# Gate and up weights of an expert: four transfers of 2 MB become two of 4 MB, with five slots recut in the second expert

## The chip, the cores and the metric

The kernel runs on one core of one Trainium2 chip. The metric is the device time of one execution in microseconds (us). Three runs of the kernel before gave 1424.24, 1423.74 and 1421.06 us; their median is 1423.74 us.

## What is computed

Two transformer blocks on 256 tokens of width 1024, all in float32. The first block has a mixer of two head groups, then a mixture of experts, then a gated projection; the second has a local attention, a recurrent branch and a feed-forward part. The change touches only the mixture of experts:

```python
def moe(u, w_router, b_router, w_gu, b_gu, w_dn, b_dn):   # top 4 of 32 experts per token
    logits = jnp.dot(xt, w_router) + b_router
    top_logit, top_e = lax.top_k(logits, TOP_K)
    gate = jax.nn.softmax(top_logit, axis=-1)
...
    def expert_block(args):
        e, xs = args
        hh = jnp.dot(xs, w_gu[e]) + b_gu[e]                # w_gu[e] is 1024 x 2048, 8 MB
        glu, lin = jnp.split(hh, 2, axis=-1)
        glu = jnp.minimum(glu, SWIGLU_LIMIT)
        lin = jnp.clip(lin, -SWIGLU_LIMIT, SWIGLU_LIMIT)
        act = glu * jax.nn.sigmoid(SWIGLU_ALPHA * glu) * (lin + 1.0)
        return jnp.dot(act, w_dn[e]) + b_dn[e]             # w_dn[e] is 1024 x 1024, 4 MB
```

Every expert's 12 MB of weights are read once from HBM, 384 MB for the 32 experts.

## The kernel before

All weights, from the first projection to the last, come through one list, `plan` (L176 to L218), filled by `want(key, source, shape)`. An entry is a chunk of at most 2 MB: 128 partitions with 16 KB each. A chunk needs a slot of 16 KB per partition. There are ten slots: ring `a` has three, which live through the whole kernel, `b0` to `b4` have one each and live from the end of the attention (`cb`) to the end of the experts, and `c` and `d` have one each during the experts. `load_next(ring)` (L222) takes the next entry of the plan and issues its transfer on SP's DMA queue into a tile of that ring; `done(key)` (L255) is called in the code behind the last matmul that reads a chunk, and loads the next entry into the ring that the chunk had. SP executes its transfers in order; each waits, by semaphores, for the matmuls that still read the slot, and for the transfer eight before it on the same semaphore.

In the experts an entry `("gu", e, c)` is a quarter of the gate and up weights of expert e (two row blocks of 2048 columns, in one run of 16 KB per partition), `("dn", e, c)` a half of the down weights. The plan's order is gu of expert e, then dn of expert e-1. The last six transfers of the experts keep out of ring `a` (L226), so that its three slots take the weights of the next stage (`pg`, `in2`) as soon as the plan is there. Ring `d` is given up after expert 10, since the path for overfull experts (`past_slots`) and a table for the second block use its memory.

PE's order in the experts is written out by hand (`manual_schedule`, L1210): `up(e+1)`, that is four quarters of 16 matmuls each, with the scatter of expert e-1 behind the first two and the gates of expert e+2 behind the third; then the first half of `down_part(e)`, the transposes of `glu(e+1)` (tile `tr`), the gather of the tokens of expert e+2 (tile `xg`), and the second half of `down_part(e)`. ACT and DVE do the activation between. This hand-written order ends behind `up(E - 1)`; the last calls of `down_part` and `glu` are placed by a scheduler:

```python
        h1 = up(e + 1, aside)
        if e == E - 2:
            break
...
    order.close()
    i = down_part(E - 2, aT, 0)
    with tc.issue_after(i.ins):
        aL = glu(E - 1, h1)
    down_part(E - 2, aT, 1)
    down_part(E - 1, aL, 0)
    i = down_part(E - 1, aL, 1)
```

In the rows, tile `gu` is the PSUM result of `up` (L1086), `y` that of `down_part` (L1122, one PSUM bank), `w` any weight chunk, `gl` the activation that `down_part` reads, `h` the copy of `gu` that the transposes read. A quarter of `up` is 16 matmul records, a half of `down_part` too.

Of the kernel before, what the change touches and what calls it, by code (L numbers as in the profile page):

```python
# [25 lines left out]
FT = mybir.dt.float32  # L26
# [10 lines left out]
P = 128  # L37
S = 256
D = 1024
E = 32  # L40
# [64 lines left out]
def block_kernel(ctx: ExitStack, tc: tile.TileContext, A, out, dbg=None, parts=("t1", "moe", "over", "t3")):  # L105
# [70 lines left out]
    plan = []  # L176

    def want(key, ap, shape):
        plan.append((key, ap, shape))
# [10 lines left out]
    want(("o", 0), wo[0], [P, 4, 1024])  # L190
    fd = dram.tile([8, 384], FT, name="fd")
    wg, wd = A["w_gu"], A["w_dn"]
    for e in range(E + 1):
        if e < E:
            for c in range(4):
                want(("gu", e, c), wg[e, c], [P, 2, 2048])
                if (e, c) == (1, 0):
                    want(("pp",), A["w_pp"].rearrange("(k p) n -> p k n", p=P), [P, 2, 1024])
        if e > 0:
            for c in range(2):  # L200
                want(("dn", e - 1, c), wd[e - 1, c], [P, 4, 1024])
        if e == E_REL:
            want(("R",), bass.AP(tensor=fd.tensor, offset=fd.offset, ap=[[1, P], [1, 2944]]), [P, 2944])
# [9 lines left out]
    for j in range(11):  # L213
        want(("up", j), A["w_up"][j], [P, 2, 2048])
        if j % 2 == 0:
            n = min(4, 22 - 2 * j)
            want(("down", j // 2), A["w_down"][j * 256:j * 256 + n * P].rearrange("(k p) n -> p k n", p=P),
                 [P, n, 1024])  # L218
    state = {"next": 0, "held": 0, "d": True}
    live = {}  # L220

    def load_next(ring):  # L222
        i = state["next"]
        if i >= len(plan) or (ring != "a" and i >= stop_moe) or (ring == "d" and not state["d"]):
            return
        if ring == "a" and stop_moe - 6 <= i < stop_moe:  # L226

            state["held"] += 1
            return
        state["next"] = i + 1  # L230
        key, ap, shape = plan[i]
        t = rings[ring].tile([P, 4096], FT, name="w")
        n = int(np.prod(shape[1:]))
        v = t[:, :n]
        if len(ap.shape) == 3:
            v = v.rearrange("p (a b) -> p a b", b=ap.shape[2])
        if i == 0:
            for h in range(2):
                SY.dma_start(v[:, h], ap[:, h])
        elif key == ("dn", E - 1, 1):  # L240
            for h in range(2):
                SY.dma_start(v[:, 2 * h:2 * h + 2], ap[:, 2 * h:2 * h + 2])
        else:
            SY.dma_start(v, ap)
        if key == ("R",):
            SY.dma_start(t[0:E, 3072:3072 + D], A["b_dn"])
        live[key] = (t, ring)
        if i + 1 == stop_moe:
            for _ in range(state["held"]):
                load_next("a")  # L250

    def W(key):
        return live[key][0]

    def done(key):  # L255
        load_next(live.pop(key)[1])

    for _ in range(NRING_A):
        load_next("a")
# [749 lines left out]
    held = {}  # L1009
# [167 lines left out]
    def past_slots():  # L1177
# [7 lines left out]
        with tc.If(mv > CAP):  # L1185
            for t in range(2):
# [7 lines left out]
                with tc.For_i(0, E, 1) as e:  # L1194
                    cv = nc.values_load(cnti[0:1, ds(e, 1)], min_val=0, max_val=S)
                    with tc.If(cv > CAP):
                        V.tensor_copy(gc, gover[:, t, ds(e, 1)])
                        V.tensor_copy(bg, bgu[:, ds(e, 1), :].rearrange("p o n -> p (o n)"))
                        for m in range(8):
                            for s in range(2):  # L1200
                                for c in range(4):
                                    G.dma_start(w[:, 2 * c:2 * c + 2],
                                                 wg[ds(e, 1), c, :, :, s * 1024 + m * P:s * 1024 + (m + 1) * P]
                                                 .rearrange("o p k n -> p (o k) n"))
                                for k in range(8):
                                    PE.matmul(pacc[:, s * P:(s + 1) * P], w[:, k], uT[:, k], start=(k == 0), stop=(k == 7))
                            ts(gl, pacc[:, 0:P], bg[:, m:m + 1], 7.0, OP.add, OP.min)
                            act(sg, gl, AF.Sigmoid, scale=1.702)
                            ts(li, pacc[:, P:2 * P], bg[:, 8 + m:9 + m], 7.0, OP.add, OP.min)
                            ts(li, li, -7.0, 1.0, OP.max, OP.add)  # L1210
                            tt(gl, gl, sg, OP.mult)
                            tt(aT[:, m], gl, li, OP.mult)
                        for s in range(8):
                            for c in range(2):
                                G.dma_start(w[:, 4 * c:4 * c + 4], wd[ds(e, 1), c, :, :, s * P:(s + 1) * P]
                                             .rearrange("o p k n -> p (o k) n"))
                            for k in range(8):
                                PE.matmul(pacc[:, 0:P], aT[:, k], w[:, k], start=(k == 0), stop=(k == 7))
                            hs = xn[:, t, s * P:(s + 1) * P]
                            stt(hs, pacc[:, 0:P], gc, hs, OP.mult, OP.add)  # L1220
# [517 lines left out]
def host_arrays(inputs):  # L1738
# [46 lines left out]
    f["g_post_ffn"] = c(g["g_post_ffn_2"])  # L1785
    f["g_pre_ffn"] = c(g["g_pre_ffn_2"])

    f["w_gu"] = c(g["w_gu"][0].reshape(E, 4, 2, P, 2 * D).transpose(0, 1, 3, 2, 4))
    f["w_dn"] = c(g["w_dn"][0].reshape(E, 2, 4, P, D).transpose(0, 1, 3, 2, 4))
    f["b_gu"] = c(g["b_gu"][0].reshape(E, 16, P).transpose(2, 0, 1))  # L1790
    f["b_dn"] = c(g["b_dn"][0])
# [59 lines left out]
```

## Time and profile before

| | |
|---|---|
| median of three runs | 1423.74 us |
| the profiled execution's own time | 1422.5 us |
| its span, first to last instruction | 1420.5 us |
| mean granted TensorE clock | 0.987 of full speed |
| PE busy | 1315.2 us (93%) |
| DVE busy | 627.6 us (44%) |
| ACT busy | 371.8 us (26%) |
| bytes by DMA | 482.40 MB, mean 340 GB/s |

The span is cut into 40 slices of 35.5 us on the profile's page. Slices 1 to 4 are the first block's mixer, the experts fill slices 5 to 30, the second block the rest. PE's share counts every issued matmul as busy for its modelled length, so it says nothing about whether a stage waits for data; the chain of work that ended last says that.

### The profile page before, as it was taken

The numbers are of one execution on the slowest core, as the hardware profiler recorded it, in microseconds if no ns is written. First come the engines' busy times: TensorE is split into PE (matmuls) and PEld (weight loads), VectorE is DVE, ScalarE is ACT, GpSimd is POOL, SyncE is SP. The second block draws the span as 40 slices with busy tenths as digits, with TensorE's granted clock in tenths as the row PEclk, the third lists the DMA queues.
The fourth block names the chain that finished last, engine by engine and source line by source line (L and its number), as shares of the span: only waits on it lengthen the run. The fifth ranks groups of instructions, "written<-read, shape, count | busy, mean of one in ns | idle before, by whom it ended". The sixth has DMA issues, their size and how long they took to land.

```text
span 1420.5 us, 19855 instructions
## 1 busy us (share of the span) xinstructions
PE 1315.2 (93%) x8393; PEld 744.0 (52%) x8394; DVE 627.6 (44%) x1250; ACT 371.8 (26%) x641; POOL 40.0 (3%) x54
## 2 busy tenths in 40 slices
PE   8989999999998888889998888988888998999997
PEld 7777543434333333333343333333335886899997
DVE  6766532332322232222232222322226878677776
ACT  5654211101100010001110001100014658555554
POOL 1010200000000000000000000000000101000000
PEclk9999999999999999999999999999999999999999
DMA  7366899999999999999999999999998523355530
GB/s 287 112 239 270 340 427 427 426 427 426 427 427 427 427 427 426 425 412 427 427 427 427 427 428 427 427 426 427 427 426 350 188 103 134 138 196 197 196 149 31
DMA packets 40591, 482.40 MB, mean 340 GB/s; under 512 B 4104, under 2 KB 4640, under 8 KB 12592
## 3 DMA queue, kind: packets, MB, share of 16 engines
q1 hardware_dynamic: 39232, 477.99, 81.2%
q0 software_dynamic: 832, 2.62, 0.6%
q8 instruction: 68, 1.11, 0.3%
q10 hardware_dynamic: 432, 0.46, 0.1%
q14 instruction: 27, 0.22, 0.0%
HBM read 479.99 MB, written 1.06 MB: 339 GB/s over the span
## 4 chain that ended last, share of the span: by engine, by line
DMA 47%; PE 45%; DVE 4%; issue 2%; ACT 2%; POOL 1%; DVEq 0%; ACTq 0%; SPq 0%; POOLq 0%
DMA w<-w_gu 25%; DMA w<-w_dn 19%; PE gu L1086 10%; PE y L1122 4%; PE acc L289 3%; PE acc L290 3%; PE acc L291 3%; PE wk L290 3%; PE wk L291 3%; PE wk L289 3%; DMA w<-w_pg 2%; PE pj L289 1%; PE pj L291 1%; PE pj L290 1%; PE xg L1056 1%
## 5 line engine op out<-in xcount | busy, mean ns | idle before, releaser
L1086 PE MATMUL gu<-w,xg 128*64 128x512 f32 x2048 | 470.1, 601 | 45.2 <-DMA w<-w_gu 39.1
L1086 PEld LDWEIGHTS gu<-w,xg 128*64 128x64 f32 x2048 | 141.6, 137 | 315.4 <-issue 249.8
L1122 PE MATMUL y<-w,gl 128*64 128x512 f32 x1024 | 233.1, 597 | 28.9 <-DMA w<-w_dn 27.2
L121 ACT ACTIVATE h<-gu,gs 128x512 f32<-128x512 f32 x64 | 40.5, 683 | 558.8 <-PE gu L1086 558.8
L124 DVE TENSOR_TENSOR h<-sc,h 128x512 f32<-128x512 f32 x126 | 81.4, 686 | 201.0 <-PE sc L1146 198.5
L273 DVE TENSOR_TENSOR wl<-w,wh 128x1024 fp32r<-128x1024 f32 (+2 forms) x124 | 147.5, 1200 | 45.5 <-ACT wh L121 45.0
L1122 PEld LDWEIGHTS y<-w,gl 128*64 128x64 f32 x1024 | 73.5, 136 | 161.3 <-issue 157.9
L121 ACT ACTIVATE wh<-w 128x1024 fp32r<-128x1024 f32 (+2 forms) x125 | 128.2, 1038 | 91.0 <-PE acc L291 21.6
L124 DVE TENSOR_TENSOR gl<-tr,bgu 128x512 f32<-128x512 f32 x32 | 22.1, 692 | 270.1 <-PE tr L1101 270.1
L290 PE MATMUL wk<-ul,wh 128*128 128x256 f32 x336 | 94.5, 281 | 0.2 <-DVE ul L124 0.2
L289 PE MATMUL wk<-uh,wh 128*128 128x256 f32 x336 | 94.5, 281 | 0.0
L291 PE MATMUL wk<-uh,wl 128*128 128x256 f32 x336 | 94.3, 281 | 0.0
L121 ACT ACTIVATE sg<-gl 128x512 f32<-128x512 f32 x32 | 20.1, 629 | 183.0 <-DVE gl L131 183.0
L290 PEld LDWEIGHTS wk<-ul,wh 128*128 128x128 f32 x336 | 63.4, 189 | 1.2 <-DVE ul L124 0.4
L1071 DVE CAST gt<-y 128x256 fp32r<-128x256 f32 x32 | 13.6, 424 | 114.0 <-PE y L1069 114.0
L289 PEld LDWEIGHTS wk<-uh,wh 128*128 128x128 f32 x336 | 63.3, 188 | 1.0 <-ACT uh L121 0.2
L291 PEld LDWEIGHTS wk<-uh,wl 128*128 128x128 f32 x336 | 63.4, 189 | 0.0
L1056 PE MATMUL xg<-oh,u 128*128 128x64 bf16 x1536 | 50.0, 193 | 0.7 <-ACT proj L121 0.7
L1056 PEld LDWEIGHTS <-u 128*128 128x128 bf16 x1536 | 49.1, 98 | 2.6 <-issue 2.3
L127 DVE SCALAR_TENSOR_TENSOR cv<-wk,vec,cv 128x255 f32<-128x255 f32 x88 | 42.3, 480 | 8.7 <-ACT cv L121 7.1
L127 DVE SCALAR_TENSOR_TENSOR sg<-y,gs,li 128x512 fp32r<-128x512 f32 x31 | 23.3, 751 | 49.7 <-ACT li L121 49.7
L121 ACT ACTIVATE li<-y,gs 128x512 fp32r<-128x512 f32 x31 | 21.3, 687 | 80.9 <-PE y L1122 79.4
(419 smaller groups left out, 1753.3 us busy)
## 6 DMA issues: line engine op xcount, KB each, us to landing
w<-w_gu SPq DMA_DIRECT2D x128, 2048.0 KB, 39.1
w<-w_dn SPq DMA_DIRECT2D x63, 2048.0 KB, 39.1
w<-w_up SPq DMA_DIRECT2D x11, 2048.0 KB, 7.8
w<-w_in SPq DMA_DIRECT2D x7, 2048.0 KB, 9.5
w<-w_down SPq DMA_DIRECT2D x5, 2048.0 KB, 7.6
w<-w_o SPq DMA_DIRECT2D x4, 2048.0 KB, 8.6
w<-w_pg SPq DMA_DIRECT2D x2, 2048.0 KB, 35.4
w<-w_in SPq DMA_DIRECT2D x2, 1024.0 KB, 8.3
```

What stands on the lines that cost most here:

```text
L121: return SC.activation(out=o, in_=i, func=f, **kw)
L124: return V.tensor_tensor(out=o, in0=a, in1=b, op=op)
L127: return V.scalar_tensor_tensor(out=o, in0=a, scalar=s, in1=b, op0=op0, op1=op1)
L273: eng.tensor_tensor(out=lo, in0=src, in1=hi.bitcast(FT), op=OP.subtract)
L289: PE.matmul(o, l[0], r[0], start=first, stop=False)
L290: PE.matmul(o, l[0], r[1], start=False, stop=False)
L291: PE.matmul(o, l[1], r[0], start=False, stop=last)
L1056: PE.matmul(px[:, kd], u3[i][:, t, kd * P:(kd + 1) * P], oh[:, t], start=(n == 0), stop=(n == 5))
L1071: V.tensor_copy(gt, pgt[:, 0:S])
L1086: PE.matmul(ps[64 * s:64 * s + 64, n], xg[:, k], w[:, kk, s * 1024 + n * 512:s * 1024 + (n + 1) * 512], start=(k == 0), stop=(k == 7))
L1122: i = PE.matmul(ps[64 * s:64 * s + 64], aT[:, k], w[:, kk, s * 512:(s + 1) * 512], start=(k == 0), stop=(k == 7))
```

## The change

- The host lays the gate and up weights out as two halves per expert instead of four quarters. In a half a partition's four row blocks are one run of 32 KB.
- Experts 0 and 1 are still loaded by quarters through the plan (now runs of 16 KB inside the 32 KB). From expert 2 on the plan has only dn; the 60 halves are in a list of their own, `pairs_`.
- Slots `b0` to `b3` are not reloaded when expert 0 is through. Behind the first quarter of expert 1, `cb` is closed, and the memory of the five slots is recut: `p0` and `p1` of 32 KB and a new `b4` of 16 KB. `p0` takes the first halves, `p1` the second ones (`load_pair`). A half's slot comes free when both its quarters are read.
- All other slots take dn. dn of expert e may be loaded once both halves of expert e are issued; until then a free ring is put on the list `wait`, and is loaded behind the next half.
- The rule that kept the last six transfers out of ring `a` is gone.
- The path for overfull experts reads the new layout with half as many transfers. No expert is overfull here, so it does not run.

```diff
-        if e < E:
+        if e < 2:
             for c in range(4):
-                want(("gu", e, c), wg[e, c], [P, 2, 2048])
+                want(("gu", e, c), wg[e, c // 2][:, 2 * (c % 2):2 * (c % 2) + 2], [P, 2, 2048])
...
+        elif e < E:
+            pairs_ += [(e, 0), (e, 1)]
...
+    def load_pair(ring):
+        i = state["pair"]
+        if i >= len(pairs_):
+            return
+        state["pair"] = i + 1
+        e, h = pairs_[i]
+        t = rings[ring].tile([P, 8192], FT, name="w2")
+        SY.dma_start(t.rearrange("p (a b) -> p a b", b=2048), wg[e, h])
+        live["gu", e, 2 * h] = (t[:, 0:4096], None)
+        live["gu", e, 2 * h + 1] = (t[:, 4096:8192], ring)
+        again, state["wait"] = state["wait"], []
+        for r in again:
+            load_next(r)
...
     def load_next(ring):
+        if ring in ("p0", "p1"):
+            return load_pair(ring)
...
-        if ring == "a" and stop_moe - 6 <= i < stop_moe:
-            state["held"] += 1
+        k = plan[i][0]
+        if k[0] == "dn" and k[1] >= 2 and state["pair"] < 2 * (k[1] - 1):
+            state["wait"].append(ring)
             return
...
     def done(key):
-        load_next(live.pop(key)[1])
+        ring = live.pop(key)[1]
+        if ring is None or ring in ("b0", "b1", "b2", "b3"):
+            return
+        if key == ("gu", 1, 0):
+            cb.close()
+            for r in ("p0", "p1", "b4"):
+                rings[r] = pool_(cb, "ring" + r)
+                load_next(r)
+            return
+        load_next(ring)
...
-    f["w_gu"] = c(g["w_gu"][0].reshape(E, 4, 2, P, 2 * D).transpose(0, 1, 3, 2, 4))
+    f["w_gu"] = c(g["w_gu"][0].reshape(E, 2, 4, P, 2 * D).transpose(0, 1, 3, 2, 4))
```

The change moves two things that an argument about time has to look at. The first is SP's queue from expert 0 on. Before (the first `x6` are quarters of experts 0 and 1, the `x4` behind are expert 2, then 3):

```order
L244 DMA w<-w_gu 128x4096 x6
L244 DMA w<-w_dn 128x4096 x2
L244 DMA w<-w_gu 128x4096 x4
L244 DMA w<-w_dn 128x4096 x2
L244 DMA w<-w_gu 128x4096 x4
```

That is: the four quarters of expert e+1 always stand ahead of the two dn of expert e. In the changed kernel, on the same queue and from the same place:

```order
L265 DMA w<-w_gu 128x4096 x6
L265 DMA w<-w_dn 128x4096 x2
L233 DMA w_2018<-w_gu 128x8192
L233 DMA w_2023<-w_gu 128x8192
L265 DMA w<-w_dn 128x4096 x4
L233 DMA w_2194<-w_gu 128x8192
L233 DMA w_2229<-w_gu 128x8192
L265 DMA w<-w_dn 128x4096 x2
```

The two halves of expert 2 are followed by the dn of experts 1 and 2, and from then on the dn of expert e stand directly behind the halves of expert e, ahead of those of expert e+1.

The second is PE at the end of the experts, from the last matmul of the gather for expert 31. Before:

```order
L1056 MATMUL xg<-oh,u_1622 128x64
L1122 MATMUL y<-w,gl 64x512 x8
L1086 MATMUL gu<-w,xg 64x512 x8
L1146 MATMUL sc<-li,gt 128x512 x2
L1146 MATMUL sc<-sg,gt 128x512 x2
L1086 MATMUL gu<-w,xg 64x512 x8
L1146 MATMUL sc<-li,gt 128x512 x2
L1146 MATMUL sc<-sg,gt 128x512 x2
L1086 MATMUL gu<-w,xg 64x512 x16
L1122 MATMUL y<-w,gl 64x512 x8
L1101 MATMUL tr<-cf,h_7972 128x128 x8
L1122 MATMUL y<-w,gl 64x512 x24
```

Here the first `y` row is the second half of expert 29, and both halves of expert 30 stand behind `up(31)`: 8 ahead of the transposes, 8 of the 24 behind them. (One row here is two records of the trace.) In the changed kernel:

```order
L1084 MATMUL xg<-oh,u_1622 128x64
L1150 MATMUL y<-w,gl 64x512 x23
L1114 MATMUL gu<-w_7611,xg 64x512 x8
L1174 MATMUL sc<-li,gt 128x512 x2
L1174 MATMUL sc<-sg,gt 128x512 x2
L1114 MATMUL gu<-w_7611,xg 64x512 x8
L1174 MATMUL sc<-li,gt 128x512 x2
L1174 MATMUL sc<-sg,gt 128x512 x2
L1150 MATMUL y<-w,gl 64x512
L1114 MATMUL gu<-w_7646,xg 64x512 x16
L1129 MATMUL tr<-cf,h_7798 128x128 x8
L1150 MATMUL y<-w,gl 64x512 x16
```

The scheduler has put 15 of the 16 `y` matmuls of expert 30 ahead of `up(31)` and one behind its first half; behind the transposes only the 16 of expert 31 are left.

## Rows read from the trace of the kernel before

**Rows 1.** The page: busy tenths of PE and DMA, and GB/s, in 40 slices.

```profile
PE   8989999999998888889998888988888998999997
DMA  7366899999999999999999999999998523355530
GB/s 287 112 239 270 340 427 427 426 427 426 427 427 427 427 427 426 425 412 427 427 427 427 427 428 427 427 426 427 427 426 350 188 103 134 138 196 197 196 149 31
```

**Rows 2.** The page: the chain that ended last, by engine and line.

```profile
DMA 47%; PE 45%; DVE 4%; issue 2%; ACT 2%; POOL 1%; DVEq 0%; ACTq 0%; SPq 0%; POOLq 0%
DMA w<-w_gu 25%; DMA w<-w_dn 19%; PE gu L1086 10%; PE y L1122 4%; PE acc L289 3%; PE acc L290 3%; PE acc L291 3%; PE wk L290 3%; PE wk L291 3%; PE wk L289 3%; DMA w<-w_pg 2%; PE pj L289 1%; PE pj L291 1%; PE pj L290 1%; PE xg L1056 1%
```

**Rows 3.** Busy time by stretch; the last two columns are DMA share and GB/s.

```profile
core 0: us, PE busy (x) PEld busy (x) DVE busy (x) ACT busy (x) POOL busy (x), PEclk, DMA share, GB/s
...
770.00:1000.00 230.00, 205.28 (x1286) 80.48 (x1282) 65.88 (x144) 19.39 (x30) 0.00 (x0) 1.00 1.01 427
```

**Rows 4.** PE's timeline within one expert: start, length (us), instruction, idle before.

```profile
774.58 3.65 PE L1086 MATMUL gu<-w,xg 128*64 128x512 f32 x16
...
779.38 3.65 PE L1086 MATMUL gu<-w,xg 128*64 128x512 f32 x16 [0.49 <-DMA w<-w_gu]
...
803.99 2.37 PE L1086 MATMUL gu<-w,xg 128*64 128x512 f32 x10 [0.15 <-DMA w<-w_gu]
```

**Rows 5.** PE's timeline, experts 0 to 3.

```profile
163.21 3.65 PE L1086 MATMUL gu<-w,xg 128*64 128x512 f32 x16 [0.86 <-DVE xg L124]
...
167.51 7.09 PE L1086 MATMUL gu<-w,xg 128*64 128x512 f32 x32
...
175.23 3.65 PE L1086 MATMUL gu<-w,xg 128*64 128x512 f32 x16
...
205.32 3.60 PE L1086 MATMUL gu<-w,xg 128*64 128x512 f32 x16
...
209.51 3.65 PE L1086 MATMUL gu<-w,xg 128*64 128x512 f32 x16
...
213.76 3.65 PE L1086 MATMUL gu<-w,xg 128*64 128x512 f32 x16
...
221.54 3.60 PE L1122 MATMUL y<-w,gl 128*64 128x512 f32 x16
...
230.98 3.60 PE L1086 MATMUL gu<-w,xg 128*64 128x512 f32 x16
```

**Rows 6.** SP's timeline: transfers as issued, expert 2 and dn of expert 1.

```profile
166.91 12.35 SPq L244 DMA_DIRECT2D w<-w_gu  x4
184.93 3.76 SPq L244 DMA_DIRECT2D w<-w_dn  x2
```

**Rows 7.** Tile w, transfers issued from 155 to 192 us: issue to landing.

```profile
DMA to landing us min/median/max: 7.4/11.2/14.3
```

**Rows 8.** PE's timeline at the end of the experts.

```profile
1056.09 3.65 PE L1086 MATMUL gu<-w,xg 128*64 128x512 f32 x16 [1.25 <-DMA w<-w_gu]
...
1064.69 1.09 PE L1101 MATMUL tr<-cf,h 128*128 128x128 f32 x8
...
1071.19 7.09 PE L1122 MATMUL y<-w,gl 128*64 128x512 f32 x32 [1.62 <-DVE sg L127]
```

**Rows 9.** ACT's and DVE's timeline at the same place.

```profile
1059.86 1.26 ACT L121 ACTIVATE h<-gu,gs 128x512 f32<-128x512 f32 x2 [17.99 <-PE gu L1086]
...
1068.93 0.69 DVE L124 TENSOR_TENSOR gl<-gl,sg 128x512 f32<-128x512 f32 x1
...
1081.15 2.19 ACT L121 ACTIVATE wh<-w,vec 128x1024 fp32r<-128x1024 f32 x2 [2.09 <-DMA w<-w_pg]
```

**Rows 10.** Stretch and DMA packets from 1072 to 1080 us, with runs of 4 KB.

```profile
1072.00:1080.00 8.00, 7.97 (x44) 3.36 (x40) 0.75 (x1) 0.69 (x1) 0.60 (x1) 1.00 1.02 414
...
DMA packets 657, 3.31 MB, mean 414 GB/s; under 512 B 26, under 2 KB 26, under 8 KB 560
```

More of the change, by code (lines that the diff above doesn't have):

```diff
@@ L192, in block_kernel @@
     wg, wd = A["w_gu"], A["w_dn"]
+    pairs_ = []
     for e in range(E + 1):
-        if e < E:
+        if e < 2:
             for c in range(4):
-                want(("gu", e, c), wg[e, c], [P, 2, 2048])
+                want(("gu", e, c), wg[e, c // 2][:, 2 * (c % 2):2 * (c % 2) + 2], [P, 2, 2048])
                 if (e, c) == (1, 0):
                     want(("pp",), A["w_pp"].rearrange("(k p) n -> p k n", p=P), [P, 2, 1024])
+        elif e < E:
+            pairs_ += [(e, 0), (e, 1)]
         if e > 0:
@@ L218, in block_kernel @@
                  [P, n, 1024])
-    state = {"next": 0, "held": 0, "d": True}
+    state = {"next": 0, "d": True, "pair": 0, "wait": []}
     live = {}
+    def load_pair(ring):
[11 more added lines that the diff above has]
+            load_next(r)
     def load_next(ring):
+        if ring in ("p0", "p1"):
+            return load_pair(ring)
         i = state["next"]
@@ L247, in load_next @@
         live[key] = (t, ring)
-        if i + 1 == stop_moe:
-            for _ in range(state["held"]):
-                load_next("a")
     def W(key):
@@ L1200, in past_slots @@
                             for s in range(2):
-                                for c in range(4):
-                                    G.dma_start(w[:, 2 * c:2 * c + 2],
+                                for c in range(2):
+                                    G.dma_start(w[:, 4 * c:4 * c + 4],
                                                  wg[ds(e, 1), c, :, :, s * 1024 + m * P:s * 1024 + (m + 1) * P]
```

## The prediction

> **What bounds the kernel now.** I read the page's 40 slices first: DMA is full at 427 GB/s from slice 6 to slice 30, while PE, at 88 or 89%, is not [rows 1]. The chain agrees: the transfers of w_gu and w_dn are 44% of it, the largest piece [rows 2]. PE's timeline inside one expert then shows how it waits: before nearly every chunk there is a short idle time that a transfer ended, and the first quarter of one expert to that of the next lies 803.99 - 774.58 = 29.4 us, which is what 12 MB (12.58 million bytes) take at 427 GB/s, 29.5 us [rows 3, 4]. The same expert with all data there takes PE 230.98 - 205.32 = 25.66 us [rows 5]. So in the experts the end is set by when DMA's stream began, by its rate, and by what PE still has to do when the stream has brought the last chunks. The change touches all three. In the rest of the kernel PE, DVE and ACT set the time, and the change leaves that code as it is.
>
> **The rate.** At 427 GB/s, 2 MB (2.097 million bytes) take 4.91 us, a half of 4 MB 9.82 us; each of the 16 engines brings a run of 16 KB in 16 x 16384 / 427 = 613.9 ns [rows 3]. What a run costs beside its bytes is read from a stretch with shorter runs: from 1072 to 1080 us DMA is as full (share 1.02) and brings 414 GB/s [rows 10]. Of its 657 packets 560 are under 8 KB, 26 of these under 512 B; 534 runs of 4 KB are 2.19 of the 3.31 MB. If the other 1.12 MB went at 427, the 4 KB runs went at 408 GB/s, 160.7 ns each. From 4 to 16 KB it is then (613.9 - 160.7) / 3 = 151.1 ns per 4 KB, and 9.7 ns are left per run. A run of 32 KB would take 8 x 151.1 + 9.7 = 1218 ns where two take 1228. With 8 such runs per engine a half saves 78 ns, and the 58 halves that stream behind the recut save **4.5 us**. Bounds: nothing, if 32 KB are brought in two pieces; and the double, 9 us, since the stretch is short. I take 4.5.
>
> The Trainium skill, page "DMA: Bandwidth & Descriptors", section "Bandwidth", puts a ceiling of 435.2 GB/s on the 16 ports. If the longer runs reached it, a half would take 9.64 instead of 9.82 us the 58 halves would save 10.8 us, and the sum below would be 1431.0. The trace doesn't show that it is reached: the full stretch stays at 427.
>
> **The start of the stream.** Before, the first quarter of expert 2 is issued when the first slot of expert 0 comes free: 163.21 + 3.65, issued 166.91 [rows 5, 6]. Its earliest landing is 7.4 us after issue, 4.91 of it transfer, so 2.5 us pass without data of its own [rows 7]. In the changed kernel `p0` covers `b0` and `b1`. In the built program SP's transfer waits for the readers of that memory, not for the place in the code where `cb` is closed, so the first half of expert 2 can be issued when the second quarter of expert 0 is read: 167.51 + 7.09/2, about 171.0, that is **4.1 us** later. The second half follows when the fourth quarter is read, 175.23 + 3.65 = 178.9, while the first streams. Then dn of experts 1 and 2 follow, slots coming free with each quarter of expert 1. The stream so runs from about 173.2 for 2 x 9.82 + 4 x 4.91 = 39.3 us, until 212.5. The next half, for expert 3, must wait until both quarters of expert 2's first half are read, and PE is busy up to then without a wait: 209.51 + 3.65 = 213.16 [rows 5]. With 2.5 us up to its first data DMA stands for about **3 us**. Before, SP had the slots to keep it full there [rows 1]. Sum at the start: 7 us.
>
> After that I find no further hole. A half landed at A is read at A + 7.8 (205.32 to 213.16 [rows 5]); behind it are queued the other half, until A + 9.8, and two dn, until A + 19.6. The new half is issued 11.8 us ahead of the end of the queue, and needs 2.5. The second half is issued at A + 17.6, when there is a queue until A + 29.5. Six slots of 16 KB, five after expert 10, hold dn of two experts and part of a third.
>
> **The end of the experts.** Before, the stream ends with the four dn of experts 30 and 31. The last quarter of expert 31 starts on PE at 1056.09 as it lands; four chunks are left, so the stream ends at T = 1056.0 + 4 x 4.91 = 1075.7. The last `y` matmul ends at 1071.19 + 7.09 = 1078.28, T + 2.6 [rows 8]: PE does dn 30 and nearly all of its other work while the stream still runs.
>
> In the changed kernel dn 30 is in its slots early, and the last 4 MB of gate and up land only two chunks ahead of the end. Let the first half of expert 31 land at A; the second lands at A + 9.8, the stream ends at T' = A + 19.6. PE by its new order: the last half of expert 30 landed at A - 19.6 (between lie two dn and a half); its two quarters with the gates take 221.54 - 213.76 = 7.8, down, transposes, gather and down 230.98 - 221.54 = 9.4 [rows 5], so PE is at A - 2.4. Now the 15 moved matmuls: their PSUM bank must first be emptied, 1.6 us of idle as before expert 31 [rows 8], which gives A - 0.8, and 15/16 of 7.09 us bring A + 5.9. Only then do the first two quarters of expert 31 start, with the scatter 8.4 us (205.32 to 213.76), one `y` matmul 0.2, then the last two quarters, which have long landed, 7.1: A + 21.6. Nothing covers what follows: about 0.8 us until ACT has copied the first half of `gu` (1.26 us for both [rows 9]), the transposes and the activation, 1064.69 to 1069.62 = 4.9 us [rows 8, 9], and 7.09 + 0.1 for the last dn. That is A + 34.5 = T' + 14.9, where it was T + 2.6. Cost: **12.3 us**. Without the moved matmuls it would be 11.5: the second half lands 9.8 us ahead of the end, 7.0 for its quarters, 16.7 for the two dn, the transposes and the bank.
>
> What comes behind: the loads of `pg` are now issued as slots of ring `a` come free, the first behind dn 31, the second only when dn 30 is read. PE's own tail is so long that both land before it is over; before, ACT waited 2.1 us for `pg` [rows 9]. I set no gain for that, since PE waited for the sums of DVE there in any case. The smaller program of POOL isn't executed: nothing.
>
> **Sum** against the profiled execution, 1422.5 us: + 7 + 12.3 - 4.5 = + 14.8, that is **1437.3 us**. The profiled one lies 1.2 us below the median of three runs, well within their spread, so I add nothing.
>
> **Rivals.**
> 1. The runs of 32 KB bring nothing: + 19.3, 1441.8 us. For it: no row shows a run above 16 KB. Against: short runs do cost [rows 10]. 14%.
> 2. The tail stays covered, because in the real queue the dn of expert 31 is still what PE waits for last. Then only the start and the rate count: + 2.5, 1425. It decides if the last `y` again ends within 3 us of the last landing. Against: the order of the last two chunks leaves PE 34 us of work and 20 us of stream. 5%.
> 3. It gets faster: each transfer takes a fixed piece out of the stream, and 60 fewer of them give more than the 19.3 us back. It decides from 19.3 / 58 = 0.33 us per half. The 2.5 us of issue and landing beside 4.91 of transfer [rows 7] would give 58 x 2.5 = 145 us, 1278 us, if none of it were covered. Against: with transfers of 2 MB back to back DMA's share is 1.01 at 427 GB/s, so there is no piece between them to win [rows 3]. 3%. The Trainium skill states such a piece: "DMA: Bandwidth & Descriptors", section "Anatomy of one DMA", about 2.0 us per transfer, measured for GpSimd's path; 60 fewer would then be worth 120 us, a time of 1321.8 us. The full stretch here speaks against its being paid in a stream.
> 4. Two slots of 4 MB are too few, and DMA runs dry once per expert. A hole like that at expert 3, 3 us for 28 experts, gives 84 us more, 1521. It decides if PE releases a half over 9 us later than I work out. Against: PE needs 25.66 us for an expert and DMA 29.5. 4%.
>
> **How the numbers follow.** My forecast with the saving at work has 74%. The predicted time is 1437.3. For the range I take rival 1 in, with 3 us for the start and the tail: 1445 above; below, a saving of 9 us and 3 us for the start and the tail: 1430. Left out are rivals 2 to 4, 12%, and some of the edges. A measurement of this kernel can tell about 0.2%, 2.9 us, from no change. Rival 3 is faster, 3%; rival 2 is the same, 5%; all else slower, 92%.
>
> **What would show it.** Right: the halves' first transfer issued near 171 us, and a hole in DMA between 212 and 216 us; then a full stream whose GB/s lie at 429; the last `y` matmul 14 to 16 us behind the last landing of dn 31, with 15 `y` matmuls ahead of the first quarter of expert 31; from there to the end the same length as before, within 2 us. Wrong: GB/s still 427 (rival 1) or above 440 (rival 3), PE ending with the stream (rival 2), or DMA idle in every expert (rival 4).

## The result and the profile after

| | before | after |
|---|---|---|
| median of the runs, us | 1423.74 (3) | 1442.26 (3: 1439.98 to 1442.48) |
| profiled execution: time, span, us | 1422.5, 1420.5 | 1442.5, 1440.3 |
| mean granted clock of TensorE | 0.987 | 0.969 |
| last 32 matmuls of the experts begin, end, us | 1071.19, 1078.28 | 1089.25, 1097.74 |
| last down weights land, us | 1075.8 | 1079.2 |
| from the last matmul of the experts to the end of the span, us | 342.2 | 342.6 |

The changed kernel is slower: ratio 1.0135, 95% interval 1.0121 to 1.0149. The forecast was 1437.3 us, range 1430 to 1445. All of the loss is there when the last matmul of the experts ends: 19.5 of 19.8 us of span. What comes behind it is as long as before.

Two rows of the page of the changed kernel, in 40 slices:

```profile
PEclk9999999999999999999999999999998999999999
GB/s 283 111 240 268 316 395 426 431 425 428 433 430 430 426 431 432 414 429 424 392 435 426 433 424 432 430 428 427 428 424 191 176 153 132 132 180 198 203 151 30
```

Against [rows 1] slices 5 and 6 are down from 340 and 427 to 316 and 395 GB/s (the start), the middle is up by some 2 GB/s, and PEclk has one slice of 8, at the end of the experts. Stretches cut to the events show it more sharply (busy time by stretch; the last three columns are PEclk, the granted clock of TensorE with 1.00 for full speed, DMA share and GB/s):

```profile
core 0: us, PE busy (x) PEld busy (x) DVE busy (x) ACT busy (x) POOL busy (x), PEclk, DMA share, GB/s
165.00:173.00 8.00, 8.00 (x42) 2.97 (x40) 0.88 (x4) 0.00 (x0) 0.00 (x0) 1.00 0.45 164
173.00:212.00 39.00, 39.00 (x278) 16.32 (x276) 12.16 (x29) 5.76 (x8) 0.00 (x0) 1.00 0.98 417
212.00:216.00 4.00, 4.00 (x22) 1.29 (x20) 1.29 (x2) 0.00 (x0) 0.00 (x0) 1.00 0.61 188
...
770.00:1000.00 230.00, 211.79 (x1312) 83.43 (x1308) 65.84 (x144) 20.66 (x32) 0.00 (x0) 0.96 1.00 429
...
1086.00:1093.00 7.00, 3.75 (x12) 1.42 (x14) 2.58 (x5) 1.32 (x2) 0.00 (x0) 0.56 0.14 54
```

The late start (164 GB/s up to 173 us) and the hole behind 212 us are where the prediction put them, and the stream runs at 429 where it ran at 427 [rows 3]. SP's timeline has the halves as they were issued; the first two rows answer to [rows 6]:

```profile
171.85 8.05 SPq L233 DMA_DIRECT2D w<-w_gu  x2
185.57 11.49 SPq L265 DMA_DIRECT2D w<-w_dn  x4
213.86 8.87 SPq L233 DMA_DIRECT2D w<-w_gu  x2
```

The end on PE's timeline, which answers to [rows 8]:

```profile
1029.90 5.35 PE L1114 MATMUL gu<-w,xg 128*64 128x512 f32 x16 [2.20 <-DMA w<-w_gu]
...
1059.07 6.65 PE L1150 MATMUL y<-w,gl 128*64 128x512 f32 x29 [1.58 <-DVE sg L127]
...
1074.92 7.45 PE L1114 MATMUL gu<-w,xg 128*64 128x512 f32 x31
1083.21 1.24 PE L1129 MATMUL tr<-cf,h 128*128 128x128 f32 x8 [0.84 <-ACT h L121]
1089.25 8.49 PE L1150 MATMUL y<-w,gl 128*64 128x512 f32 x32 [4.80 <-issue]
```

Read from the bottom: the last 32 `y` matmuls stand behind 4.80 us in which PE has nothing, and take 8.49 us where they took 7.09. The last wait of PE that a transfer ended is the one at 1029.90, 68 us ahead of the end. The 29 `y` matmuls of expert 30 at 1059.07 stand ahead of the gate and up matmuls of expert 31, which is the new order. The transposes wait 0.84 us for the copy of `gu`.

When the last down weights land is read from their transfers: the last is issued at 1045.32 before and at 1051.90 in the changed kernel, and takes the longest time to landing of the two in its row (before, then after):

```profile
DMA to landing us min/median/max: 28.3/29.4/30.4
DMA to landing us min/median/max: 25.2/26.2/27.3
```

With the record's further digit (30.44 and 27.29 us) that is 1075.76 and 1079.19. PE ends 2.51 us behind it before, and 18.55 us behind it in the changed kernel.

### The profile page after: what moved, and what is told of

Read it like the earlier page. It is cut to its first block, busy times and chain, and to the rows that moved or that the text cites. A ratio compares the mean times of both kernels' runs of the same rounds, so it can differ in the third digit from the quotient of the medians.

```text
span 1440.3 us, 19689 instructions
## 1 busy us (share of the span) xinstructions
PE 1335.2 (93%) x8393; PEld 750.3 (52%) x8394; DVE 628.1 (44%) x1250; ACT 372.3 (26%) x641; POOL 40.0 (3%) x54
## 3 DMA queue, kind: packets, MB, share of 16 engines
HBM read 479.99 MB, written 1.06 MB: 334 GB/s over the span
## 5 line engine op out<-in xcount | busy, mean ns | idle before, releaser
L1114 PE MATMUL gu<-w,xg 128*64 128x512 f32 x2048 | 494.4, 626 | 66.1 <-DMA w<-w_gu 62.0
L1114 PEld LDWEIGHTS gu<-w,xg 128*64 128x64 f32 x2048 | 149.1, 142 | 350.2 <-issue 273.1
L124 DVE TENSOR_TENSOR gl<-tr,bgu 128x512 f32<-128x512 f32 x32 | 22.1, 692 | 217.0 <-PE tr L1129 217.0
L127 DVE SCALAR_TENSOR_TENSOR sg<-y,gs,li 128x512 fp32r<-128x512 f32 x31 | 23.3, 751 | 49.4 <-ACT li L121 49.2
```

The source lines that it names most:

```text
L124: return V.tensor_tensor(out=o, in0=a, in1=b, op=op)
L127: return V.scalar_tensor_tensor(out=o, in0=a, scalar=s, in1=b, op0=op0, op1=op1)
L1114: PE.matmul(ps[64 * s:64 * s + 64, n], xg[:, k], w[:, kk, s * 1024 + n * 512:s * 1024 + (n + 1) * 512], start=(k == 0), stop=(k == 7))
```

## Experiments

Ratios are to the kernel before, run beside each kernel on the same chip. Each is sure to 0.1 to 0.2%, so what lies between two ratios is sure to about 3 us; where that is too coarse, a trace of each kernel decides. Diffs are against the changed kernel unless another is named.

**1. Down of expert 30 late.** One condition, which makes the two down transfers of expert 30 wait for all halves of gate and up, as in the kernel before:

```
-        if k[0] == "dn" and k[1] >= 2 and state["pair"] < 2 * (k[1] - 1):
+        if k[0] == "dn" and k[1] >= 2 and state["pair"] < min(2 * E - 4, 2 * (k[1] - 1) + 2 * (k[1] >= E - 2)):
```

> The changed kernel, with one thing different: dn of expert 30 is queued behind both halves of expert 31 instead of ahead of them (the scheduler then also puts its matmuls back behind up(31)). Theory: most of the loss is the uncovered tail, because the last gate and up weights land only two chunks ahead of the stream's end. Then the last y matmul ends 4 to 5 us behind the stream's end instead of 19, a hole of about 1 us opens in DMA before the halves of expert 31, and the time falls by 13 to 14 us: ratio to the kernel before about 1.004. Rival: the loss lies along the whole stream (two slots are too few, PE waits 2 us and falls to the lower clock in every expert). Then the order of two chunks at the end changes at most 2 us: ratio 1.012 to 1.0135.

Measured: 1432.96 us, ratio 1.0074 (1.0060 to 1.0088); the last `y` ends 9.7 us earlier than in the changed kernel. The order was the largest part of the tail, but some 4 us are missing from what was expected: PE ends 7.8 us behind the last landing, not 4 to 5. A stretch and PE's timeline of this kernel show two reasons:

```profile
1000.00:1040.00 40.00, 38.57 (x214) 14.12 (x214) 10.63 (x20) 2.58 (x4) 0.00 (x0) 0.93 0.95 398
```

```profile
1038.62 3.65 PE L1114 MATMUL gu<-w,xg 128*64 128x512 f32 x16 [1.06 <-DMA w<-w_gu]
...
1080.99 7.09 PE L1150 MATMUL y<-w,gl 128*64 128x512 f32 x32 [1.57 <-DVE sg L127]
```

The halves of experts 30 and 31 now follow one another with nothing between, and with two large slots each must wait until the half two places ahead is read: 398 instead of 426 GB/s for 40 us, 2.6 us. And from 1038.62 PE waits for no data any more; the two experts in a row leave it behind the stream, and the end hangs on PE.

**2. PE's order by hand at the end.** The line that ends the scheduler's freedom moves behind the last product, so PE keeps the written order, with expert 30's `y` behind expert 31's gate and up:

```
-    order.close()
...
     i = down_part(E - 1, aL, 1)
+    order.close()
```

> The changed kernel with its own queue, but PE's last matmuls in the order of the kernel before, written by hand: both halves of dn 30 behind up(31). Theory: the stream still brings the last half late, so most of the tail stays; what goes is the time that the moved matmuls put ahead of up(31), the uncovered emptying of their bank and the lower clock behind the idle time: from 19 us between the stream's end and the last y matmul to 14, 4 to 5 us less in all, ratio about 1.010. Rival: the scheduler's new order is the whole loss at the end; then the tail is as before and 16 us go, ratio 1.002.

Measured: 1436.17 us, ratio 1.0100 (1.0085 to 1.0116), as expected. Between the two ratios lie 0.35%, 5.0 us, and the last `y` ends at 1092.56, 5.2 us earlier than in the changed kernel. So much of the loss is the order in which PE takes what has landed, with what hangs on it (the emptying of the bank and the clock), without any change of a transfer. PE now waits for the first half of expert 31:

```profile
1059.13 3.65 PE L1114 MATMUL gu<-w,xg 128*64 128x512 f32 x16 [2.89 <-DMA w<-w_gu]
```

The last down weights land at 1078.61, so the tail is 13.95 us.

**3. The moved matmuls kept, the stall behind them filled.** Expert 30's `y` stands ahead of expert 31's gate and up by hand, its bank is emptied behind the activation of expert 31, and 20 bf16 matmuls into a free bank, whose results nobody reads, run where PE stood for 4.8 us:

```
+    warm = pg_.tile([P, 2, 512], FT, name="gu")
...
+    for _ in range(20):
+        PE.matmul(warm[:, 0], onesb, u3[0][:, 0, 0:512], start=True, stop=True)
```

> The changed kernel with PE's last matmuls in its own order by hand (the 16 of dn 30 together ahead of up(31)), and 20 matmuls into a free bank between the transposes of expert 31 and its y matmuls, whose result nobody reads. Theory: 1.4 us of the tail are the lower clock, to which PE falls in the idle time before the last y matmuls; with PE busy there the 32 records of y take 7.1 us instead of 8.5. Rival: those matmuls are slow for another reason (a transfer, a bank), and still take 8.5. In the time it is 1 to 2 us, at the edge of what a ratio can tell: 1.012 against 1.0135.

Measured: 1437.83 us, ratio 1.0113 (1.0097 to 1.0128). PE's timeline:

```profile
1081.71 4.48 PE L1293 MATMUL gu<-u,onesb 128*128 128x512 bf16 x19
1086.63 7.09 PE L1150 MATMUL y<-w,gl 128*64 128x512 f32 x32 [0.44 <-DVE sg L127]
```

The last product is back at 7.09 us, and PEclk is 1.00 from 1080 to 1094 us (0.56 from 1086 to 1093 in the changed kernel). The two ratios lie 3.1 us apart, which is no more than they are sure to. The rows show 1.4 us of it, the clock in the last product; the rest isn't told apart from the order by hand.

**4. The slots cut anew in expert 9 instead of 1.** The five small slots serve experts 0 to 9, and the new ones are cut only when all five are empty:

```
+    CUT = 10
-        if e < 2:
+        if e < CUT:
...
-        if key == ("gu", 1, 0):
+        if ring[0] == "b" and state["old"] and state["next"] >= stop_b:
```

> The changed kernel with the five slots recut at expert 10 instead of expert 2: experts 0 to 9 come by quarters through ten slots, as before, when the stream has long been full. Theory: the start costs 7 us (first transfer 4 us late, a hole of 3 us before expert 3), and the recut costs nothing where transfers wait in line; 16 halves fewer gain 78 ns each, 1.2 us. So 5.8 us less than the changed kernel: ratio about 1.0095, no hole in DMA from 170 us on. Rival: wherever the slots are recut, four of them stand empty until it is done, and the same 7 us are lost there: ratio 1.014, and a stretch near 410 to 430 us in which DMA is idle.

Measured: 1436.93 us, ratio 1.0097 (1.0082 to 1.0113), as expected. The start, and the place of the recut, by stretch:

```profile
165.00:216.00 51.00, 51.00 (x334) 20.59 (x332) 14.32 (x35) 5.76 (x8) 0.00 (x0) 1.00 0.99 415
...
400.00:460.00 60.00, 43.38 (x278) 17.35 (x276) 13.14 (x28) 5.16 (x8) 0.00 (x0) 0.86 1.01 431
```

Both are full. Between the ratio of the change and this one lie 5.4 us, although 16 halves go in short runs again; with 16 x 78 ns for these the start was worth 6.6 us. The landings agree: counted from the first gate and up matmul of the experts, the down weights of expert 10 land 5.9 us earlier than in the changed kernel.

**5. The order of before, throughout.** Recut in expert 9, every down behind both halves of the next expert, the last expert's halves in two transfers of 2 MB each. Against the kernel of experiment 4:

```
-        if k[0] == "dn" and k[1] >= CUT and state["pair"] < 2 * (k[1] - CUT + 1):
+        if k[0] == "dn" and k[1] >= CUT and state["pair"] < min(2 * (E - CUT), 2 * (k[1] - CUT + 2)):
...
+        n = 2 if e == E - 1 else 1
```

> The slots are cut anew only in expert 9, the down halves of every expert from 10 on stand behind both gate and up halves of the next expert (the order of the kernel before), and the last expert's two halves go in two transfers of 2 MB each; everything else as changed. Theory (the rate gain is real, and the loss of the change was only its late start, the order of its last transfers and the coarse last halves): the stream ends 44 halves x 78 ns = 3.4 us earlier than in the kernel before and the tail is the one of before, so the ratio is 0.9976 (0.996 to 0.999), with 429 GB/s and a DMA share of 1.00 from 770 to 1000 us and no stretch at a lower share from 300 to 1070 us but the one that the kernel before has too. Rival (slots of 32 KB cost by themselves: with only two of them a half cannot be issued before the half two places ahead has been read, and the DMA engines run dry now and then): a share below 1.00 between 770 and 1000 us and a ratio of 1.000 or more.

Measured: 1435.59 us, ratio 1.0096 (1.0082 to 1.0111). A miss, by some 17 us. By stretch:

```profile
420.00:460.00 40.00, 33.45 (x190) 12.76 (x192) 9.09 (x20) 2.58 (x4) 0.00 (x0) 0.85 0.89 372
560.00:700.00 140.00, 118.93 (x674) 45.48 (x676) 36.34 (x77) 12.53 (x20) 0.00 (x0) 0.89 0.92 386
770.00:1000.00 230.00, 207.04 (x1310) 82.23 (x1308) 65.15 (x143) 20.65 (x32) 0.00 (x0) 0.98 1.01 430
```

In the steady stretch the stream is full, against the rival as it was put. But the DMA engines run dry at the two disturbances: behind the recut (372 for 427 GB/s over 40 us, 5.2 us) and around the load of `R` (386 where before had 422 over 140 us, 11.9 us). Together 17.1 us, less the 3.4 us of the rate, is close to the 13.2 us measured between the medians (11.6 at the last `y` of this execution). With the order of the change the same recut costs nothing (experiment 4, 431 GB/s there). That each expert's down right behind its own halves keeps the queue longer where something is late is read from the order, and was not tried by itself. SP's longest wait around `R`, 24.9 us, is for PE to read a half. PE begins that half at 680.33, behind 9.7 us of matmuls on what the load of `R` brought, and from 680 to 690 us the stream is down to 169 GB/s. With the same work and the order of the change the stream is not dry there (423 GB/s in experiment 4).

**6. The same with a coarse end.** `n = 1`: the last halves in one transfer each.

> The kernel of e6_old_order with the last expert's halves in one transfer of 4 MB each, as in the change. Theory (the end hangs on TensorE's work behind the landing of the last gate and up quarter or half: 22 us in the kernel before, of which one quarter's 4.3 us become a half's 7.9): 3.6 to 3.8 us slower than e6_old_order, ratio 1.0002 (0.9990 to 1.0015). Rival (the last down halves land late enough to cover it): the ratio of e6_old_order within 0.001.

Measured: 1435.46 us, ratio 1.0097 (1.0082 to 1.0111). The totals don't tell: around `R` this kernel brought 398 GB/s where experiment 5 brought 386, 3.9 us more over 140 us. The ends do. First the kernel of experiment 5, then this one:

```profile
1067.79 3.65 PE L1122 MATMUL gu<-w,xg 128*64 128x512 f32 x16 [1.25 <-DMA w<-w_gu]
1072.78 3.65 PE L1158 MATMUL y<-w,gl 128*64 128x512 f32 x16 [1.33 <-DMA w<-w_dn]
...
1082.82 7.09 PE L1158 MATMUL y<-w,gl 128*64 128x512 f32 x32 [1.57 <-DVE sg L127]
```

```profile
1064.19 7.09 PE L1122 MATMUL gu<-w,xg 128*64 128x512 f32 x32 [0.92 <-DMA w<-w_gu]
...
1080.89 7.09 PE L1158 MATMUL y<-w,gl 128*64 128x512 f32 x32 [1.58 <-DVE sg L127]
```

From the landing of the last gate and up data, which PE waits for, to the end of the last `y` it is 1089.91 - 1067.79 = 22.1 us with quarters and 23.8 with halves. The coarse end costs 1.7 us and not 3.7: with quarters PE then waits for down of expert 30 anyway (1.33 us).

**7. Runs or transfers?** Three kernels ask where 429 GB/s come from. The first has the slots and order of experiment 5 with all halves in two transfers of 2 MB (`n = 2`), so runs of 16 KB.

> The kernel of e6_old_order, but every half of gate and up goes in two transfers of 2 MB with runs of 16 KB, so that slots, order and landing of quarters stay and run length and number of transfers go back. Theory (length of runs sets the rate): 427 GB/s from 770 to 1000 us and the time of the kernel before, ratio 1.000 (0.9985 to 1.0015). Rival (number of transfers sets the rate): the same numbers; the two are told apart by e11_runs32_64p. Rival (neither does, and 429 GB/s come from the order or the slots): 429 GB/s and the ratio of e6_old_order.

Measured: ratio 1.0046 (1.0033 to 1.0059), and 427 GB/s:

```profile
560.00:700.00 140.00, 119.62 (x690) 45.74 (x688) 37.51 (x81) 12.72 (x20) 0.00 (x0) 0.91 0.96 401
770.00:1000.00 230.00, 204.58 (x1300) 81.29 (x1302) 65.46 (x140) 20.44 (x32) 0.00 (x0) 1.00 1.01 427
```

The rate is as the theory has it; the time is not, because of the dry stretch around `R` (401 for 422, 7.0 us). The second was to keep the runs of 32 KB and double the transfers, by splitting the 128 partitions:

```
-        SY.dma_start(t.rearrange("p (a b) -> p a b", b=2048), wg[e, h])
+            SY.dma_start(t[64 * q:64 * q + 64].rearrange("p (a b) -> p a b", b=2048), wg[e, h][64 * q:64 * q + 64])
```

> The kernel of e6_old_order, but every half of gate and up of the experts before the last goes in two transfers of 2 MB, one for each 64 partitions, with runs of 32 KB: as many transfers as in e10_runs16, the runs of e6_old_order. Theory (length of runs): 429 GB/s from 770 to 1000 us, ratio 0.9976 like e6_old_order within 0.001. Rival (number of transfers): 427 GB/s and a ratio of 1.000 like e10_runs16.

Measured: 1973.23 us (1925 to 2037), ratio 1.3879 (1.3821 to 1.3937). It says nothing on the question, and something else instead (last section). The third is the changed kernel with weights laid out in quarters, so that one transfer of 4 MB carries runs of 16 KB:

```
-        SY.dma_start(t.rearrange("p (a b) -> p a b", b=2048), wg[e, h])
+        SY.dma_start(t.rearrange("p (q x) -> p q x", q=2), wg[e, 2 * h:2 * h + 2].rearrange("q p a b -> p q (a b)"))
```

> The changed kernel with the weights laid out in quarters as before, so that one transfer of 4 MB for a half carries runs of 16 KB: the number of transfers, slots and order of the change, the runs of before. Theory (length of runs sets the rate): 427 GB/s from 770 to 1000 us and, with 58 halves x 78 ns = 4.5 us more, a ratio of 1.0166 to the kernel before (1.015 to 1.018). Rival (number of transfers sets the rate): 429 GB/s and the ratio of the changed kernel, 1.0135 within 0.0015.

Measured: 1444.60 us, ratio 1.0155 (1.0139 to 1.0171), which fits both; the stretch does not:

```profile
770.00:1000.00 230.00, 209.67 (x1319) 82.73 (x1314) 65.58 (x143) 19.98 (x31) 0.00 (x0) 0.98 1.01 427
```

As few transfers as in the change, and the rate of before: it is the length of the runs. Half as many transfers for the same bytes of gate and up bring nothing in a full stream. The Trainium skill's fixed piece of about 2.0 us per transfer ("DMA: Bandwidth & Descriptors", "Anatomy of one DMA"), which the prediction weighed, is not paid there: the stream has 427 GB/s with transfers of 2 MB [rows 3] and of 4 MB.

**8. Two versions that keep the rate.** The first is the kernel of experiment 4 whose slots are cut back into five of 16 KB in expert 28 (`UNC`), so that the last three experts go as before.

```
-    CUT = 10
+    CUT, UNC = 10, 29
...
+            cb.close()
+            for q in range(5):
+                rings[f"b{q}"] = pool_(cb, f"ringb{q}")
+                load_next(f"b{q}")
```

> The changed kernel with its slots cut anew in expert 9 and cut back into five of 16 KB in expert 28, so that the last three experts go as in the kernel before. Theory (the loss lies in start and tail alone): 38 halves x 78 ns = 3.0 us from the rate, up to 3.5 us lost once where the large slots are read out and nothing may be issued until the third is free, the tail as before: ratio 1.000 (0.998 to 1.0025). Rival (large slots cost in mid-stream too): above 1.0025, with a stretch below 420 GB/s between 300 and 900 us that the kernel before has not.

Measured: 1423.78 us, ratio 1.0010 (1.0001 to 1.0019), within what was expected: start and tail give back the loss but for 1.4 us, and the second cut has its price (412 GB/s over 50 us, 2.0 us):

```profile
950.00:1000.00 50.00, 43.31 (x284) 17.45 (x285) 14.01 (x32) 5.16 (x8) 0.00 (x0) 0.93 0.98 412
```

The tail is not quite the one of before, as the expectation had it. PE waits for data for the last time at the second cut, stays behind the stream from there, and ends 7.0 us behind the last landing:

```profile
969.84 5.79 PE L1137 MATMUL gu<-w,xg 128*64 128x512 f32 x16 [6.69 <-DMA w<-w_gu]
```

The second never cuts back. It goes from the order of the change to that of before one down half at a time, so that a down half always lies between two experts; the last expert's halves go in quarters:

```
-        if k[0] == "dn" and k[1] >= CUT and state["pair"] < 2 * (k[1] - CUT + 1):
+        if k[0] == "dn" and k[1] >= CUT and state["pair"] < min(2 * (E - CUT), 2 * (k[1] - CUT + 1 + (k[1:] >= (E - 4, 1)))):
```

> The changed kernel with its slots cut anew in expert 9 (as in e5_late_recut), the order of the change up to expert 28, and then the down halves let back one at a time (one down half of expert 28 between the gates of 29 and 30, both of 29 between 30 and 31, those of 30 behind 31), so that no two experts' halves follow one another without a down half between; the last expert's halves in two transfers each. Theory (late start, order of the end, coarse end, and dry stretches where nothing lies between two experts are all of the loss): no stretch under 420 GB/s from 300 to 1070 us but the one at 560 to 700 us, TensorE's last product of the experts ends 3 us before that of the kernel before, ratio 0.9976 (0.996 to 0.9995). Rival (every move of the order with only two large slots leaves the DMA engines dry for 2 to 3 us, as moves in e1_late_dn30 and e6_old_order did): stretches below 420 GB/s between 900 and 1060 us and a ratio of 1.000 to 1.004.

Measured: 1419.53 us against 1422.37, ratio 0.9979 (0.9970 to 0.9989): **faster than both kernels**, 1.5% under the change by the two ratios. Its stretches (from 165 to 216 us it has 413 GB/s, as experiment 4 has 415) and its end:

```profile
420.00:460.00 40.00, 30.57 (x176) 11.85 (x178) 8.29 (x18) 2.58 (x4) 0.00 (x0) 0.84 1.00 429
...
770.00:1000.00 230.00, 212.01 (x1322) 83.74 (x1318) 65.05 (x142) 20.65 (x32) 0.00 (x0) 0.97 1.00 429
1000.00:1030.00 30.00, 30.00 (x190) 11.91 (x188) 9.34 (x18) 2.58 (x4) 0.00 (x0) 1.00 1.00 422
1030.00:1060.00 30.00, 30.00 (x186) 11.34 (x187) 7.91 (x16) 3.85 (x6) 0.00 (x0) 1.00 1.01 427
```

```profile
1068.32 5.37 PE L1158 MATMUL y<-w,gl 128*64 128x512 f32 x24 [1.57 <-DVE sg L127]
1073.86 1.94 PE L1158 MATMUL y<-w,gl 128*64 128x512 f32 x8 [0.17 <-DMA w<-w_dn]
```

None of these stretches is dry (from 1060 to 1070 us it is 417 GB/s, a little under what was expected, with 419 in the kernel before; around `R` it is 417 for 422), and the last eight matmuls wait for the last transfer itself: the end hangs on the stream again, and ends at 1075.8, 2.5 us ahead of before. With all four causes that the expectation names taken away at once the time is as expected, and the rival's dry stretches are not there. How much each of the four gave here is not told apart.

## Why the prediction came out

**The sign and the place were right, the size was 4 to 5 us short.** The forecast was + 14.8 us against the profiled execution; measured are + 20.0 there and + 18.5 between the medians. Step by step:

- **Start, + 7.** The first half is issued at 171.85. This execution is 0.65 us late from the first gate and up matmul on (163.86 for 163.21 [rows 5]), so that is 171.2 where 171.0 was worked out. The hole lies at 212 to 216 us, at 188 GB/s. Experiment 4 measured 6.6 us.
- **Rate, - 4.5.** 429 GB/s, as the prediction said would show it. In the trace's DMA records a run of 32 KB has a median of 1216 ns, one of 16 KB 613 (estimated 1218 and 613.9). Over a long stretch less came: from the landing of one half to that of another 25 experts on, the changed kernel took 1029.90 - 286.04 = 743.86 us and the kernel of short runs in experiment 7 1032.04 - 285.62 = 746.42. That is 2.6 us for 50 halves or 51 ns each, 3.0 us for 58, from one execution of each. The step was right in kind, and some 1.5 us too large.
- **Start and rate together, + 2.5.** The stream ends at T' = 1079.2, 3.4 us after the T of before. Without this execution's late start that is 2.8.
- **Tail, + 12.3.** This is the term that was mis-sized: it measured 16.0. The last `y` ends at T' + 18.55 where T' + 14.9 was worked out, beyond the 14 to 16 us that were to show the forecast right; before, it was T + 2.51. The price of the moved `y` matmuls of expert 30 is what failed. The prediction put the tail without them at T' + 13.9 (9.8 us ahead of the end, then 7.0 and 16.7; the 11.5 that it names for the cost should be 11.3), and experiment 2, which has them back, measured 13.95. Moving them was to add about 1 us; the two tails lie 4.6 us apart, 0.6 of it from a fall of the clock ahead of the moved matmuls.

PE's rows place the 3.7 us by which the tail is longer than worked out. The second half of expert 30 is issued at 1018.31 and lands 21.2 us later at 1039.5; PE begins it only at 1040.10, 0.6 us late, without waiting, because its matmuls at 1029.90 ran at the lower clock (below). In experiment 1 PE is there in time and waits 1.06 us. From there to the moved matmuls it is 19.0 us where 18.8 were worked out: 0.2. The gate and up of expert 31 end at 1082.37, 23.3 us behind the start of the moved matmuls, and not 22.4: 0.9. From the transposes' start to that of `y` it is 6.04 us and not 4.9: 1.1. The 32 `y` matmuls take 8.49 us: 1.4. The stream's last part took 0.5 us longer than worked out, which counts the other way. The order of the steps and what covers what were right.

Two things were not seen ahead: the emptying of a bank, and the clock. The bank of expert 30's `y` is emptied only behind the activation of expert 31; both use the tiles `li` and `sg`, of which there is one buffer each. ACT and DVE:

```profile
1087.59 0.69 ACT L121 ACTIVATE li<-y,gs 128x512 fp32r<-128x512 f32 x1 [0.76 <-DVE gl L127]
```

```profile
1087.59 0.69 DVE L124 TENSOR_TENSOR gl<-gl,sg 128x512 f32<-128x512 f32 x1
1088.39 0.75 DVE L127 SCALAR_TENSOR_TENSOR sg<-y,gs,li 128x512 fp32r<-128x512 f32 x1
```

The last `y` needs that bank, so it starts at 1089.25 behind the `sg` of 1088.39 and not behind the `gl` of 1087.59. In experiment 3 the last `y` waits for the same `sg` by its row. The clock cost 2.0 of the 3.7 us, 0.6 at the start of the tail and 1.4 at its end (last section).

**The rivals.** Rival 1 (no gain by long runs) gives 1441.8, nearer to the median than the forecast; the total alone would have chosen it. That the time fell into the range owes something to this, since the range was drawn to take rival 1 in. The stretch at 429 GB/s and the third kernel of experiment 7 exclude it: a missing gain and a longer tail of the same size look alike in one number. Rival 2 (the tail stays covered) falls with the 18.55 us between the last landing and the end. Rival 3 (a fixed piece per transfer) falls with experiment 7; its 1278 us leave out the 19.3 us of start and tail and should be 1297. Rival 4 (dry once per expert) falls with the share of 1.00 in mid-stream, but its mechanism is real: a half waits for the half two places ahead. It showed wherever the order of transfers left nothing between (experiment 1) or something came late (experiment 5).

## What to carry to other kernels

Larger transfers change three things besides their rate: when the first can start (its slot needs all of the old ones under it), what the last one leaves uncovered, and how early the next can be issued. Price the gain as the bytes in the stream times the difference of the time that a byte takes, here 3.0 us measured, and hold it against one start and one tail, here 6.6 and 16.0 us. Price the tail from the order of the matmuls that the kernel will have: some 4 of the 16.0 us came with the 16 that the scheduler moved. Where the gain is wanted all the same, cut the slots when other slots keep the queue full, and order the last transfers so that the last thing to land has the least work behind it, moving pieces one at a time.

## What was not expected of the hardware

**Runs into 64 partitions took twice as long.** In experiment 7, with one transfer for each half of the partitions, one behind the other on the same queue, the DMA engines were as busy as ever:

```profile
770.00:1000.00 230.00, 146.84 (x808) 55.88 (x808) 42.05 (x91) 15.29 (x24) 0.00 (x0) 0.79 0.98 248
```

A share of 0.98 for 248 GB/s, where 128 partitions have 1.01 for 430 (experiment 5); a run of 32 KB has a median of 2508 ns in the records and not 1216. Busy engines are no proof of bytes. A third of the stream's bytes, the down weights, still go into 128 partitions. The Trainium skill, "DMA: Bandwidth & Descriptors", section "The descriptor swizzle", says that partitions 0 to 63 are written through the even ports and 64 to 127 through the odd ones. By that a transfer into 64 partitions has half of the ports; doubled runs agree with it, and no run here separates the ports from the engines.

**The clock at the end.** The last 32 matmuls stand behind 4.80 us in which PE has nothing, and the granted clock from 1086 to 1093 us is 0.56, a mean between its two levels of 1.2 and 2.4 GHz (0.5 and 1.0): 8.49 us instead of 7.09. With matmuls in that gap (experiment 3) it stays at 1.00 and they take 7.09.

In mid-stream the clock falls as well. At 1029.90, behind a wait of 2.20 us, 16 matmuls take 5.35 us and not 3.65. PE mostly has time to spare there, but this was its last wait for data, and 0.6 of the 1.7 us came through to the end. The length of the wait alone does not decide: in experiment 2's kernel the same 16 matmuls take 3.65 us behind a wait of 2.89 (its row at 1059.13). What else decides was not tried. With the halves in quarters the steady stretch has a PEclk of 1.00, in the kernel before [rows 3] and in the first kernel of experiment 7; with whole halves it is 0.96 to 0.98 in the changed kernel and in experiments 4, 5 and 8.
